# A fused attention step whose first gate stage is put in another order

## The chip, the cores and the metric

The kernel runs on one core of a Trainium2 chip. The metric is the device time of one execution in microseconds (us), the median over runs. TensorE (PE in the profile; PEld is its weight load), VectorE (DVE), ScalarE (ACT) and GpSimd (POOL) each work through a queue of their own in order; SyncE (SP) issues most of the transfers (DMA). A semaphore wait holds up everything behind it on the same engine.

## The reference, cut to what matters

One layer of a diffusion backbone: a modulated RMSNorm, one projection whose columns go to two groups of heads, two attentions, gates, an output projection.

```python
shift, scale, gate = modulation(c, w_mod[l], b_mod[l])           # silu(c) @ w_mod + b_mod
h = rmsnorm(xs, norm_gain[l]) * (1.0 + scale) + shift
q_a, k_a, v_a, g_a, q_b, k_b, v_b, g_b = project(h, w_in[l], ...)  # h @ w_in, then split
...
xs = xs + gate * merge_out(o_a, g_a, o_b, g_b, w_out[l])         # (o * silu(g)) @ w_out
```

There are 1152 tokens of width 1024: 128 context tokens (tile 0) and 1024 latent ones (tiles 1 to 8, 128 tokens each). The change concerns only the first piece of work: the norm, the modulation, and the products that give `g_a`, the gates of the first group.

## The kernel before, in words

Products are made nearly exact in three parts. A weight block of 128 rows and 512 columns, `raw` k (k from 0 to 7, named rawga in the trace), is split into a rounded high part (whiga, a cast on ACT) and the rest (wloga, a subtraction). Values h are split likewise: a high part by ACT, `h(0)`, then an exact copy hf by DVE and a low part by POOL, `h(1)`. A product is high by high, low weight by high, and high by low value.

The first stage goes over the rows of the inner dimension in steps. Step j prepares slice j of the modulation and the values, and multiplies with slice k = j - 1:

- A tile of tokens is loaded (xn), squared with its sum on ACT (sq, `squares`), the reciprocal root is taken on POOL (rsx), the tile is scaled on DVE (`scaled`), turned by eight transposes on PE (px, `turned_tile`), and copied to xT (`keep`: the first half on ACT, the second on DVE). Tiles 1 to 4 are done before the steps, the others inside them: 5 and 6 in steps 1 and 2, then 7, 8 and 0 by the table `rest`.
- `modulate_rows(j)` multiplies the slice wm of `w_mod` with the conditions (pm, 16 matmuls) and copies the rows (mrows); `modulate(j)` turns them (2 matmuls, L374) and makes the scale a_mod and the shift b_col.
- `modulated(j, 1, 4, 0)` makes the values of slice j for tiles 1 to 4 from xT (L433 on ACT, L436 on DVE, L437 on POOL). `modulated(k, 5, 2, 0)` does so for tiles 5 and 6, and the table `second` gives those of tiles 7, 8 and 0.
- `first_gates` multiplies four column groups (ch 0 to 3) with tiles 1 to 4 into four banks (pg_f, 512 wide; L267, L271, L272); `next_gates` those of tiles 5 and 6 (pg_s, 256 wide) from step 3 on.

`W_GA.split` makes both parts of one weight block and then issues the load of a later block; there are three buffers for raw blocks, three for wm and four for tiles, so a load waits until the buffer's last reader is done. All loads stand in one list on SP. `warm(n)` issues matmuls that nobody reads. The order of each engine's queue is the order in which the code is written: `in_order` at the end fixes it.

After this stage come the other projections and the attention, which hold most of the time and which the change leaves as they are.

Of the kernel before, what the change touches and what calls it, by code (L numbers as in the profile page):

```python
# [13 lines left out]
ALU = mybir.AluOpType  # L14
# [4 lines left out]
P = 128  # L19
D = 1024  # L20
KT = D // P
# [37 lines left out]
QUERY_AT = (0, 2, 3, 6)  # L59
PAD = 2  # L60
SECOND_FROM = 5
WARM = (12, 5, 2, 2, 4)
LOADLEAD = 5
OUTRATE = 2.5
PADRATE = 3
POOL_LO = ("gb",)
# [49 lines left out]
def hybrid_step(ctx, tc, x_prompt, x_sample, cache_k_a, cache_v_a, cache_k_b, cache_v_b,  # L116
# [3 lines left out]
    nc = tc.nc  # L120
# [94 lines left out]
    class Weights:  # L215
# [19 lines left out]
            for _ in range(sum(n for _, n in set(self.pools))):  # L235
                self.load()

        def split(self, eng=None):
            k = len(self.hi)
            h = wp.tile([P, 512], F32R, tag="whi", name=f"whi{self.tag}_{k}")  # L240
            l = wp.tile([P, 512], F32R, tag="wlo", name=f"wlo{self.tag}_{k}")
            nc.scalar.copy(h, self.raw[k])
            eng = eng or (nc.gpsimd if self.tag in POOL_LO and k % 2 else nc.vector)
            eng.tensor_tensor(l, self.raw[k], h, op=ALU.subtract)
            self.hi.append(h)
            self.lo.append(l)
            self.load()

    W_QA = Weights([(CQ[0], 512)], "qa")
    W_QB = Weights([(CQ[1], 512)], "qb")  # L250
# [10 lines left out]
    def gate_products(out, w, ch, ts, k, first=True, last=True, part=None):  # L261
        cs = slice(P * ch, P * ch + P)
        if part != 1:
            gate_high(out, w, cs, ts, k, first)
        if part != 0:
            i, to = third(ts)
            nc.tensor.matmul(out, w.hi[k][:, cs], h_at(1, i, k, to), start=False, stop=(k == KT - 1 and last))  # L267
# [54 lines left out]
    with tc.tile_pool(name="st", bufs=2, side="right") as st:  # L322
# [9 lines left out]
        def load_wm(j):  # L332
            w = st.tile([P, KT, 2, P], F32, tag="wm", name=f"wm{j}", bufs=3)
            for ks in (slice(0, 4), slice(4, 8)) if j == 0 else (slice(0, 8),):
                nc.sync.dma_start(w[:, ks], w_mod_ss[j][:, ks])
            wm.append(w)
# [20 lines left out]
        def modulate_rows(j, half=2):  # L357
            if half != 1:
                pmod[j] = bank_tr(f"pm{j}")
            pm = pmod[j]  # L360
            for k in range(4 * (half == 1), 4 if half == 0 else KT):
                a = 32 * (k % 4)
                nc.tensor.matmul(pm[a : a + 32, 0:256], sil32[:, k, :], wm[j][:, k].rearrange("p s n -> p (s n)"),
                                 start=(k < 4), stop=(k >= 4), tile_position=(0, a))
            if half == 0:
                return
            mrows[j] = st.tile([P, 256], F32, tag="mrows", name=f"mrows{j}")
            (nc.scalar.copy if j > 1 else nc.vector.tensor_copy)(mrows[j], pm[:, 0:256])

        def modulate(j):  # L370
            pm = pmod.pop(j)[:, 256:512]
# [17 lines left out]
        def load_x(t):  # L389
            xe[t] = st.tile([P, D + 32], F32, tag="xn", name=f"xn{t}", bufs=4)  # L390
            xn[t] = xe[t][:, 0:D]
            nc.sync.dma_start(xn[t], x_tile[t])
# [17 lines left out]
        def turned_tile(t, tags, between=None):  # L410

            for c in range(2):
                px[t, c] = bank(tags[c], f"px{t}_{c}")
                for i in range(4):
                    if c and i == 2 and between:
                        between()
                    k = 4 * c + i
                    nc.tensor.transpose(px[t, c][:, P * i : P * i + P], xn[t][:, P * k : P * k + P], ident)

        def keep(t, c, copy, a=0, b=4):  # L420
            at = slice(P * place(t), P * place(t) + P)
            copy(xT[:, 4 * c + a : 4 * c + b, at], px[t, c].rearrange("p (k n) -> p k n", n=P)[:, a:b])

        def modulated(j, t0, n, cond):

            w = P * n
            dst = slice(P * place(t0), P * place(t0) + w)
            i, to = third(dst)
            a, b = (x[:, j, cond : cond + 1] for x in (a_mod, b_col))
            hf = st.tile([P, 512], F32, tag="hf", name=f"hf{j}_{t0}", bufs=3)  # L430
            h = h_at(0, i, j, to)
            s = w // 2 if (j, t0) == (0, 1) else w
            nc.scalar.activation(h[:, 0:s], xT[:, j, dst][:, 0:s], AF.Identity, scale=a, bias=b)  # L433
            if s < w:
                nc.vector.tensor_scalar(h[:, s:w], xT[:, j, dst][:, s:w], a, b, op0=ALU.mult, op1=ALU.add)
            nc.vector.tensor_scalar(hf[:, :w], xT[:, j, dst], a, b, op0=ALU.mult, op1=ALU.add)  # L436
            nc.gpsimd.tensor_tensor(h_at(1, i, j, to), hf[:, :w], h_at(0, i, j, to), op=ALU.subtract)  # L437

# [3 lines left out]
        load_wm(0)  # L442
        W_GA.load()
        load_wm(1)
        load_x(5)
        W_GA.load()
        load_x(6)
        load_wm(2)
        W_GA.load()
        load_wm(3)  # L450

# [3 lines left out]
            for _ in range(n):  # L455
                nc.tensor.matmul(idle, blank, blank.unsqueeze(1).to_broadcast([P, 4, P]), start=True, stop=True)

        second = [x for k in range(KT) for x in ((k, 7, 2, 0), (k, 0, 1, 1))]

        def first_gates(ch, k, part=None):  # L460
            gate_products(big[ch], W_GA, ch, slice(0, 512), k, part=part)

        def next_gates(ch, k):
            o = 256 * (ch % 2)
# [32 lines left out]
        keep(2, 1, copies[1])  # L497
        keep(3, 1, copies[0])
        modulate_rows(0)
        W_GA.split(nc.gpsimd)  # L500
        turned_tile(4, "AB", lambda: modulate(0))
        keep(4, 0, copies[0], 0, 1)
        modulated(0, 1, 4, 0)
        keep(4, 0, copies[0], 1, 4)
        keep(4, 1, copies[1])
        load_x(7)
        squares(5)
        warm(WARM[4])
        big = [bank("ABAB"[ch], f"pg0_{ch}_f") for ch in range(4)]
        sg_tile.append(lambda n: st.tile([P, 512], F32, tag="sg", name=n))  # L510
        rest = {3: 7, 4: 8, 5: 0}

        late = {1: 8, 2: 0}

        for j in range(1, KT + 3):
            big_on, small_on = j <= KT, 3 <= j
            if 1 < j < KT:
                W_GA.split()
            if j == KT + 1:
                put_gates(big[0], 0, 0, slice(0, 512))  # L520
            if j == 1:
                for part in (W_GA.hi, W_GA.lo):
                    for ch in range(3):
                        nc.tensor.matmul(big[ch], part[0][:, P * ch : P * ch + P], h_at(0, 0, 0, slice(0, 512)),
                                         start=(part is W_GA.hi), stop=False)
            elif big_on:
                first_gates(0, j - 1, 0)
                first_gates(1, j - 1, 0)
                if j == KT:
                    first_gates(2, j - 1, 0)  # L530
            if j == 3:
                small = [bank("C", f"pg0_{ch}_s") for ch in (0, 2)]
            if j < KT:
                modulate_rows(j)
                if j + 3 < KT:
                    load_wm(j + 3)
                if j in late:
                    load_x(late[j])
            if j in (1, 2):
                scaled(4 + j)  # L540
            if j == 1:
                W_GA.split()
            if j in rest:
                scaled(rest[j])
            if j + 1 in rest:
                squares(rest[j + 1])
            if big_on:
                first_gates(0, j - 1, 1)
                first_gates(1, j - 1, 1)
                first_gates(2, j - 1, 1 if j in (1, KT) else None)  # L550
            if j < KT:
                modulate(j)
                modulated(j, 1, 4, 0)
                if j == 1:
                    squares(6)
            if big_on:
                first_gates(3, j - 1)
            if j in (1, 2):
                turned_tile(4 + j, ("CC", "DE")[j - 1])
                for c in range(2):  # L560
                    keep(4 + j, c, copies[c])
            if j == 2:
                for k in range(2):
                    modulated(k, 5, 2, 0)
            if j in rest:
                turned_tile(rest[j], "DE")
                for c in range(2):
                    keep(rest[j], c, copies[c])
            if 1 < j < KT:
                modulated(j, 5, 2, 0)  # L570
            for ch in range(4):
                if small_on:
                    next_gates(ch, j - 3)
                if j > SECOND_FROM or (j == SECOND_FROM and ch % 2):
                    more()
            if KT - 2 <= j < KT:
                raw = st.tile([P, KT, 2, P], F32, tag="wm", name=f"raw_qa{j}", bufs=3).rearrange(
                    "p (k a) s n -> p k (a s n)", a=2)
                k0 = 4 * (j - KT + 2)
                c0, n = W_QA.cols[0]  # L580
                nc.sync.dma_start(
                    raw, w_in[P * k0 : P * k0 + 512, c0 : c0 + n].rearrange("(k p) n -> p k n", p=P))
                W_QA.raw += [raw[:, k] for k in range(4)]
# [902 lines left out]
```

## Time and profile before

| what | value |
|---|---|
| median of 3 runs | 704.12 us (702.76 to 704.14) |
| the profiled execution | 705.18 us, span of its instructions 703.5 us |
| PE busy | 693.2 us, 99% of the span |
| DVE, ACT, POOL busy | 464.3, 410.7, 338.5 us |
| PE share of the chain that ended last | 94% |

The profile's times count from the first instruction. A row of its timeline gives start, duration, engine, line, operation, output and inputs, and in brackets how long the engine had stood idle and what it waited for. A row of the chain gives start, length and the work that decided. "PEclk" is the share of its full clock that PE was granted.

### The profile page before, as it was taken

The numbers are of one execution on the slowest core, as the hardware profiler recorded it, in microseconds if no ns is written. First come the engines' busy times: TensorE is split into PE (matmuls) and PEld (weight loads), VectorE is DVE, ScalarE is ACT, GpSimd is POOL, SyncE is SP. The second block draws the span as 40 slices with busy tenths as digits, with TensorE's granted clock in tenths as the row PEclk, the third lists the DMA queues.
The fourth block names the chain that finished last, engine by engine and source line by source line (L and its number), as shares of the span: only waits on it lengthen the run. The fifth ranks groups of instructions, "written<-read, shape, count | busy, mean of one in ns | idle before, by whom it ended". The sixth has DMA issues, their size and how long they took to land.

```text
span 703.5 us, 10690 instructions
## 1 busy us (share of the span) xinstructions
PE 693.2 (99%) x3546; PEld 560.6 (80%) x3546; DVE 464.3 (66%) x1008; ACT 410.7 (58%) x850; POOL 338.5 (48%) x357
## 2 busy tenths in 40 slices
PE   8899999999999999999999999999999999999997
PEld 4578988878788889987878787888887888887876
DVE  4678247877787773757777567567675775775563
ACT  6556412312233242178787877787778778877770
POOL 4447013332222240259676654665575557456751
PEclk9899999999999999999999999999999999999999
DMA  8952273349445016431222121212221221212323
GB/s 344 396 188 89 96 283 88 84 93 297 118 122 150 1 61 192 149 113 57 82 76 91 46 83 54 66 62 76 68 76 39 69 89 46 83 53 91 98 75 121
DMA packets 53336, 78.51 MB, mean 112 GB/s; under 512 B 6952, under 2 KB 25496, under 8 KB 52384
## 3 DMA queue, kind: packets, MB, share of 16 engines
q1 hardware_dynamic: 45040, 65.86, 28.1%
q10 hardware_dynamic: 8240, 11.96, 6.4%
q8 instruction: 28, 0.46, 0.3%
q14 instruction: 28, 0.23, 0.1%
HBM read 58.63 MB, written 19.18 MB: 111 GB/s over the span
## 4 chain that ended last, share of the span: by engine, by line
PE 94%; DMA 2%; ACT 1%; DVE 1%; issue 0%; POOL 0%; ACTq 0%; DVEq 0%
PE po L1332 14%; PE pv L1254 7%; PE pv L1251 7%; PE st L1230 5%; PE pmx L941 5%; PE pv L1253 5%; PE st L1231 5%; PE pq L259 5%; PE pq L257 5%; PE pq L258 5%; PE st L1225 4%; PE pg L267 3%; PE pg L271 3%; PE pg L272 3%; PE pk L258 2%; PE pk L259 2%
## 5 line engine op out<-in xcount | busy, mean ns | idle before, releaser
L1241 POOL TENSOR_TENSOR pl<-pe,ph 128x512 fp32r<-128x512 f32 x130 | 168.7, 1299 | 134.7 <-DVE nm L997 65.5
L942 DVE TENSOR_REDUCE mx<-pmx 128x1 f32<-128x384 f32 x192 | 101.0, 552 | 55.3 <-PE pmx L941 53.1
L1233 ACT ACTIVATE pe<-st 128x512 f32<-128x512 f32 x146 | 86.9, 595 | 28.4 <-PE st L1231 27.6
L1237 ACT CAST ph<-pe 128x512 fp32r<-128x512 f32 x146 | 90.6, 621 | 4.8
L1251 PE MATMUL pv<-ph,v_hi 128*128 128x512 f32 x208 | 82.3, 396 | 0.1
L1254 PE MATMUL pv<-pl,v_hi 128*128 128x512 f32 x208 | 82.1, 395 | 0.2 <-DVE pl L1227 0.2
L997 DVE CUSTOM_DVE_ANT_0 sn<-sn,mask,nsink 128x512 f32<-128x512 f32 (+1 forms) x64 | 46.3, 724 | 42.0 <-PE sn L994 40.6
L1332 PE MATMUL po<-wo,ogh 128*128 128x512 f32 (+1 forms) x224 | 73.3, 388 | 0.0
L182 POOL TENSOR_TENSOR rs_q<-ms_q,mhalf 128x8 f32<-128x8 f32 x18 | 34.2, 1898 | 80.8 <-DVE ms_q L180 80.8
L941 PE MATMUL pmx<-kha,qt 128*128 128x384 f32 x192 | 60.4, 362 | 0.0
L1230 PE MATMUL st<-qt,kha 128*128 128x512 f32 x144 | 57.8, 402 | 0.0
L1253 PE MATMUL pv<-ph,v_lo 128*64 128x512 f32 x146 | 57.7, 395 | 0.0
L1231 PE MATMUL st<-qb,kla 68*128 68x512 f32 x144 | 57.3, 398 | 0.0
L1254 PEld LDWEIGHTS pv<-pl,v_hi 128*128 128x128 f32 x208 | 39.0, 188 | 17.5 <-DVE pl L1227 0.6
L983 ACT ACTIVATE pen<-sn,nm 128x512 f32<-128x512 f32 (+2 forms) x72 | 45.0, 627 | 6.7 <-DVE nm L997 3.3
L1226 ACT CAST ph<-st 128x512 fp32r<-128x512 f32 x62 | 36.4, 586 | 19.8 <-PE st L1225 17.8
L1332 PEld LDWEIGHTS po<-wo,ogh 128*128 128x128 f32 x224 | 41.1, 188 | 6.4 <-ACT ogh L1294 0.3
L1251 PEld LDWEIGHTS pv<-ph,v_hi 128*128 128x128 f32 x208 | 39.2, 189 | 7.6 <-issue 0.6
L1227 DVE TENSOR_TENSOR pl<-st,ph 128x512 fp32r<-128x512 f32 x62 | 42.4, 686 | 3.0 <-ACT ph L1226 2.5
L700 ACT CAST qo0q<-ptq 128x512 fp32r<-128x512 f32 x18 | 10.6, 586 | 57.9 <-PE ptq L697 57.9
L1332 PE MATMUL po<-wo,ogl 128*128 128x512 f32 (+1 forms) x112 | 43.6, 389 | 0.0
L941 PEld LDWEIGHTS pmx<-kha,qt 128*128 128x128 f32 x192 | 35.4, 190 | 4.5
(245 smaller groups left out, 1707.2 us busy)
## 6 DMA issues: line engine op xcount, KB each, us to landing
qt<-qd SPq DMA_DIRECT2D x36, 256.0 KB, 3.0
wm<-in_w_mod_ss_dram SPq DMA_DIRECT2D x7, 1024.0 KB, 12.2
qd<-qo0q ACTq DMA_DIRECT2D x36, 128.0 KB, 2.4
qd<-qo1q ACTq DMA_DIRECT2D x36, 128.0 KB, 2.4
sgl<-gd SPq DMA_DIRECT2D x35, 128.0 KB, 2.4
out_dram<-yt SPq DMA_DIRECT2D x17, 256.0 KB, 2.1
xn<-in_x_sample_dram SPq DMA_DIRECT2D x8, 512.0 KB, 6.2
wg<-in_w_mod_g_dram SPq DMA_DIRECT2D x4, 1024.0 KB, 8.7
```

The lines of the kernel that those rows point to most:

```text
L258: nc.tensor.matmul(out, h_at(0, i, k, tok), w.lo[k], start=False, stop=False)
L941: nc.tensor.matmul(pm[:, 0:384], lhs, kha[:, g, 3 * b : 3 * b + 3, :], start=True, stop=True)
L942: nc.vector.tensor_reduce(mx[:, h, b : b + 1], pm[:, 0:384], axis=AX.X, op=ALU.max)
L1230: nc.tensor.matmul(s, kh, qtile[i], start=True, stop=False)
L1231: nc.tensor.matmul(s, kl, qbtile[i], start=False, stop=True)
L1233: nc.scalar.activation(pe, s, AF.Exp)
L1237: nc.scalar.copy(ph, pe)
L1241: nc.gpsimd.tensor_tensor(pl, pe, ph, op=ALU.subtract)
L1251: nc.tensor.matmul(pv, two, ph, start=(b == 0), stop=False)
L1253: nc.tensor.matmul(pv[0:64, :], vl, ph, start=False, stop=False)
L1254: nc.tensor.matmul(pv, two, pl, start=False, stop=last)
L1332: nc.tensor.matmul(po[n, q.start], a, wo_parts[KT * n + k][lo][:, q], start=(k == KS[0] and p == 0), stop=(k == KS[-1] and p == 2))
```

## The change

All edits are in the first stage, and what is computed stays:

- The load of raw block 1 stands ahead of tile 5's, and wm slice 2 ahead of tile 6's.
- `split` can be made in two pieces. The first low part goes from POOL to DVE and stands behind the first values of slice 0.
- Ahead of step 1, ACT copies a piece of tile 4 before it casts weight block 0, and the two turning matmuls of slice 0 come after four of tile 4's transposes in place of six.
- The values of slice 1 are made half by ACT, half by DVE, as those of slice 0 were.
- Tiles 5 and 6 are squared and turned both in step 2; tiles 7, 8 and 0 are turned in steps 4, 5 and 6 (before: 3, 4, 5), and squared one step later, behind the values of that step.
- In step 1 the products with slice 0 are put as high, slice 1 of the modulation, low weights, low values. In step 2 all four column groups have their high and low weight products before slice 2 of the modulation.
- The rows of slice 2 are copied by DVE. The warming matmuls are 12, 6, 2, 1, 5 in place of 12, 5, 2, 2, 4.
- The order in `second` follows the tiles: those of slices 0 and 1 for tiles 7 and 8 come first.

```diff
-WARM = (12, 5, 2, 2, 4)
+WARM = (12, 6, 2, 1, 5)
...
-            (nc.scalar.copy if j > 1 else nc.vector.tensor_copy)(mrows[j], pm[:, 0:256])
+            (nc.scalar.copy if j > 2 else nc.vector.tensor_copy)(mrows[j], pm[:, 0:256])
...
-            s = w // 2 if (j, t0) == (0, 1) else w
+            s = w // 2 if j < 2 and t0 == 1 else w
             nc.scalar.activation(h[:, 0:s], xT[:, j, dst][:, 0:s], AF.Identity, scale=a, bias=b)
             if s < w:
                 nc.vector.tensor_scalar(h[:, s:w], xT[:, j, dst][:, s:w], a, b, op0=ALU.mult, op1=ALU.add)
+            if between:
+                between()
             nc.vector.tensor_scalar(hf[:, :w], xT[:, j, dst], a, b, op0=ALU.mult, op1=ALU.add)
...
-        W_GA.split(nc.gpsimd)
-        turned_tile(4, "AB", lambda: modulate(0))
-        keep(4, 0, copies[0], 0, 1)
-        modulated(0, 1, 4, 0)
+        def first_values():
+            keep(4, 0, copies[0], 0, 1)
+            W_GA.split_high()
+            modulate(0)
+
+        turned_tile(4, "AB", first_values)
+        modulated(0, 1, 4, 0, W_GA.split_low)
...
-        rest = {3: 7, 4: 8, 5: 0}
+        rest = {4: 7, 5: 8, 6: 0}
...
-            if 1 < j < KT:
+            if j == 2:
+                squares(6)
+                W_GA.split_high()
+                scaled(5)
+            elif 2 < j < KT:
                 W_GA.split()
...
+                for ch in range(3):
+                    one_gate(ch, W_GA.lo[0], False)
+                modulate(1)
+                modulated(1, 1, 4, 0)
+                squares(5)
             if j in rest:
                 scaled(rest[j])
+            if big_on:
+                first_gates(0, j - 1, 1)
+                first_gates(1, j - 1, 1)
+                first_gates(2, j - 1, 1 if j in (1, 2, KT) else None)
+            if 1 < j < KT:
+                modulate(j)
+            if j == 2:
+                scaled(6)
+                W_GA.split_low()
+            if 1 < j < KT:
+                modulated(j, 1, 4, 0)
             if j + 1 in rest:
                 squares(rest[j + 1])
```

On ACT, from the cast of weight block 1 in step 1 to the values of slice 2; sq5 is the square of tile 5, h0_0_2 the high values of slice 2 for tiles 1 to 4. Before:

```order
L242 CAST whiga_1_380<-rawga_1_196 128x512
L382 ACTIVATE b_col_150<-m4_1_391,colt_163 128x2
L433 ACTIVATE h0_0_1_117<-xT_174,b_col_150,a_mod_149 128x512
L401 ACTIVATE sq6_399,ms6_400<-xn6_198 128x1025
L422 COPY xT_174<-px5_0_407 128x4x128
L242 CAST whiga_2_419<-rawga_2_202 128x512
L368 COPY mrows2_438<-pm2_429 128x256
L401 ACTIVATE sq7_445,ms7_446<-xn7_342 128x1024
L433 ACTIVATE h0_0_2_118<-xT_174,b_col_150,a_mod_149 128x512
```

And now:

```order
L241 CAST whiga_1_372<-rawga_1_194 128x512
L389 ACTIVATE b_col_150<-m4_1_383,colt_163 128x2
L440 ACTIVATE h0_0_1_117<-xT_174,b_col_150,a_mod_149 128x256
L408 ACTIVATE sq5_392,ms5_393<-xn5_196 128x1025
L408 ACTIVATE sq6_403,ms6_404<-xn6_200 128x1025
L241 CAST whiga_2_408<-rawga_2_202 128x512
L440 ACTIVATE h0_0_2_118<-xT_174,b_col_150,a_mod_149 128x512
```

The square of tile 7 no longer stands ahead of the values of slice 2, and the copy of slice 2's rows has left ACT; tile 6's square now stands ahead of the cast of weight block 2.

On PE, from the last product of slice 0 to the rows of slice 2 (pm2); px5 is tile 5 being turned. Before:

```order
L267 MATMUL pg0_3_f_357<-h1_0_0_124,whiga_0_312 128x512
L418 MATMUL px5_0_407<-ident_162,xn5_194 128x128 x4
L418 MATMUL px5_1_412<-ident_162,xn5_194 128x128 x4
L271 MATMUL pg0_0_f_354<-h0_0_1_117,whiga_1_380 128x512
L272 MATMUL pg0_0_f_354<-h0_0_1_117,wloga_1_381 128x512
L271 MATMUL pg0_1_f_355<-h0_0_1_117,whiga_1_380 128x512
L272 MATMUL pg0_1_f_355<-h0_0_1_117,wloga_1_381 128x512
L363 MATMUL pm2_429<-wm2_200,sil32_172 32x256 x8
```

And now:

```order
L274 MATMUL pg0_3_f_353<-h1_0_0_124,whiga_0_319 128x512
L278 MATMUL pg0_0_f_350<-h0_0_1_117,whiga_1_372 128x512
L279 MATMUL pg0_0_f_350<-h0_0_1_117,wloga_1_374 128x512
L278 MATMUL pg0_1_f_351<-h0_0_1_117,whiga_1_372 128x512
L279 MATMUL pg0_1_f_351<-h0_0_1_117,wloga_1_374 128x512
L278 MATMUL pg0_2_f_352<-h0_0_1_117,whiga_1_372 128x512
L279 MATMUL pg0_2_f_352<-h0_0_1_117,wloga_1_374 128x512
L278 MATMUL pg0_3_f_353<-h0_0_1_117,whiga_1_372 128x512
L279 MATMUL pg0_3_f_353<-h0_0_1_117,wloga_1_374 128x512
L370 MATMUL pm2_419<-wm2_198,sil32_172 32x256 x8
```

Tile 5's transposes have left this place (they now stand with tile 6's at the end of step 2), and four more products stand ahead of pm2.

On SP, the loads behind wm slice 1; xn5 and xn6 are tiles 5 and 6. Before:

```order
L392 DMA xn5_194<-in_x_sample_dram 128x1024
L230 DMA rawga_1_196<-in_w_in_dram 128x512
L392 DMA xn6_198<-in_x_sample_dram 128x1024
L335 DMA wm2_200<-in_w_mod_ss_dram 128x2048
L230 DMA rawga_2_202<-in_w_in_dram 128x512
```

And now:

```order
L230 DMA rawga_1_194<-in_w_in_dram 128x512
L399 DMA xn5_196<-in_x_sample_dram 128x1024
L342 DMA wm2_198<-in_w_mod_ss_dram 128x2048
L399 DMA xn6_200<-in_x_sample_dram 128x1024
L230 DMA rawga_2_202<-in_w_in_dram 128x512
```

Two pairs have changed places; the load of weight block 2 behind them stands where it stood.

More of the change, by code (lines that the diff above doesn't have):

```diff
@@ L236, in load_all, with split_high, split_low, split @@
                 self.load()
-        def split(self, eng=None):
+        def split_high(self):
             k = len(self.hi)
             h = wp.tile([P, 512], F32R, tag="whi", name=f"whi{self.tag}_{k}")
+            nc.scalar.copy(h, self.raw[k])
+            self.hi.append(h)
+        def split_low(self):
+            k = len(self.lo)
             l = wp.tile([P, 512], F32R, tag="wlo", name=f"wlo{self.tag}_{k}")
[L242 to L245, printed above, removed]
+            eng = nc.gpsimd if self.tag in POOL_LO and k % 2 else nc.vector
+            eng.tensor_tensor(l, self.raw[k], self.hi[k], op=ALU.subtract)
             self.lo.append(l)
             self.load()
+        def split(self):
+            self.split_high()
+            self.split_low()
     W_QA = Weights([(CQ[0], 512)], "qa")
@@ L414, in turned_tile @@
                 for i in range(4):
-                    if c and i == 2 and between:
+                    if c and i == 0 and between:
                         between()
@@ L422, in keep, with modulated @@
             copy(xT[:, 4 * c + a : 4 * c + b, at], px[t, c].rearrange("p (k n) -> p k n", n=P)[:, a:b])
-        def modulated(j, t0, n, cond):
+        def modulated(j, t0, n, cond, between=None):
             w = P * n
@@ L444, in hybrid_step @@
         load_wm(1)
+        W_GA.load()
         load_x(5)
-        W_GA.load()
+        load_wm(2)
         load_x(6)
-        load_wm(2)
         W_GA.load()
@@ L456, in warm, with one_gate @@
                 nc.tensor.matmul(idle, blank, blank.unsqueeze(1).to_broadcast([P, 4, P]), start=True, stop=True)
-        second = [x for k in range(KT) for x in ((k, 7, 2, 0), (k, 0, 1, 1))]
+        second = [(0, 7, 2, 0), (1, 7, 2, 0), (0, 0, 1, 1), (1, 0, 1, 1)]
+        second += [x for k in range(2, KT) for x in ((k, 7, 2, 0), (k, 0, 1, 1))]
         def first_gates(ch, k, part=None):
             gate_products(big[ch], W_GA, ch, slice(0, 512), k, part=part)
+        def one_gate(ch, w, first):
+            nc.tensor.matmul(big[ch], w[:, P * ch : P * ch + P], h_at(0, 0, 0, slice(0, 512)), start=first, stop=False)
         def next_gates(ch, k):
@@ L506, in hybrid_step @@
         load_x(7)
-        squares(5)
         warm(WARM[4])
@@ L521, in hybrid_step @@
             if j == 1:
[L522 to L525, printed above, removed]
+                for ch in range(3):
+                    one_gate(ch, W_GA.hi[0], True)
             elif big_on:
[L527 to L530, printed above, removed]
+                for ch in range(4 if j == 2 else 2 + (j == KT)):
+                    first_gates(ch, j - 1, 0)
             if j == 3:
@@ L538, in hybrid_step @@
                     load_x(late[j])
-            if j in (1, 2):
-                scaled(4 + j)
             if j == 1:
                 W_GA.split()
+                for ch in range(3):
+                    one_gate(ch, W_GA.lo[0], False)
+                modulate(1)
+                modulated(1, 1, 4, 0)
+                squares(5)
             if j in rest:
                 scaled(rest[j])
+            if big_on:
[9 more added lines that the diff above has]
+                modulated(j, 1, 4, 0)
             if j + 1 in rest:
@@ L547, in hybrid_step @@
             if big_on:
[L548 to L559, printed above, removed]
+                first_gates(3, j - 1, 1 if j == 2 else None)
+            if j == 2:
+                turned_tile(5, "CC")
                 for c in range(2):
-                    keep(4 + j, c, copies[c])
-            if j == 2:
+                    keep(5, c, copies[c])
+                turned_tile(6, "DE")
+                for c in range(2):
+                    keep(6, c, copies[c])
                 for k in range(2):
```

## The prediction

> **What bounds the kernel now.** I read the granted clock and busy times by stretches first, then the chain of work that ended last, then the timeline of its first 40 us. The stretches show where PE, the bound, is not at work (columns: stretch, length, busy time of PE, PEld, DVE, ACT and POOL with instructions, PE's clock, the transfer engines' share, GB/s):
>
> ```profile
> 21.44:24.85 3.41, 3.41 (x28) 2.16 (x27) 1.67 (x4) 1.47 (x5) 0.94 (x2) 1.00 1.03 410
> 24.85:28.26 3.41, 1.12 (x10) 0.79 (x7) 1.52 (x4) 1.32 (x3) 0.08 (x1) 1.00 1.00 411
> 28.26:31.68 3.42, 2.83 (x12) 1.56 (x16) 2.38 (x4) 3.10 (x6) 3.04 (x5) 0.50 1.07 420
> 31.68:35.09 3.41, 3.41 (x18) 2.00 (x11) 2.13 (x2) 1.42 (x3) 2.22 (x4) 0.50 0.96 330
> 60.00:700.00 640.00, 638.69 (x3179) 523.92 (x3177) 427.54 (x936) 375.67 (x781) 311.03 (x314) 1.00 0.31 95
> ```
>
> From 60 us on PE is idle for 1.31 us in 640: whatever PE gains ahead of that comes out at the end. Ahead of it there is one hole, where PE works 1.12 us of 3.41, and behind the hole two stretches at half clock. The transfer engines are full throughout, at 410 to 420 GB/s. The chain of waits names the hole's cause:
>
> ```profile
> 14.57 12.27 DMA xn<-in_x_sample_dram
> 26.94 1.15 ACT sq L401 x2
> 28.09 0.71 ACT h L433
> 28.85 0.80 PE pg_f L271
> ```
>
> The transfer of tile 7 is issued at 14.57 and lands 12.27 us later. ACT's queue holds its square, and behind it the values of slice 2, which need nothing of tile 7. PE waits for those values. The timeline says how long, and when step 4 begins:
>
> ```profile
> 28.85 0.80 PE L271 MATMUL pg_f<-h,whiga 128*128 128x512 f32 x1 [2.88 <-ACT h L433]
> ...
> 32.59 1.21 DVE L408 TENSOR_SCALAR xn<-xn,rsx 128x1024 f32<-128x1024 f32 x1
> ...
> 35.99 1.03 PE L418 MATMUL px<-ident,xn 128*128 128x128 f32 x8
> ...
> 38.29 0.40 PE L271 MATMUL pg_f<-h,whiga 128*128 128x512 f32 x1
> ```
>
> The last row is the first product with slice 3: my mark. The two rows between price the half clock. Tile 7 was scaled at 33.80 and could be turned then; PE came to it at 35.99. So the slow clock costs at most 2.2 us; the rest of that stretch is DVE and POOL at work.
>
> A rule bears on the clock. The Trainium skill, TensorE: Matmul & The Clock Gate, Part 1, says that a free-running window of about 3.4 us is watched, that an idle window halves the clock and a busy one releases it, and that the phase differs from run to run. The trace agrees on the grid (the two stretches at 0.50 are 6.83 us together, two windows), and differs in that a window with 1.12 us of work dropped it and one with 2.83 did not release it. By this page the drop may be missing in some of the timed runs of before, and then those have 2.2 us less to lose: the sum of the second rival below.
>
> **The change, part by part.** I follow PE from its first real product to the mark. Prices of PE at full clock, from the chain's steps (start to next start):
>
> ```profile
> 35.22 0.22 PE pm L374 x2
> ...
> 36.15 0.87 PE px L418 x8
> ...
> 37.38 0.12 PE pg_s L271
> ...
> 38.45 0.23 PE pg_f L271
> ...
> 39.39 1.00 PE pm L363 x16
> ```
>
> *The first low part to DVE, the copy ahead of the cast.*
>
> ```profile
> 12.74 1.27 POOL L244 TENSOR_TENSOR wloga<-rawga,whiga 128x512 fp32r<-128x512 f32 x1 [1.24 <-ACT whiga L242]
> ...
> 13.35 0.30 ACT L382 ACTIVATE b_col<-m,colt 128x2 f32<-128x2 f32 x1 [0.70 <-DVE m L376]
> 13.37 0.67 DVE L378 TENSOR_SCALAR a_mod<-m,bsc,colt 128x2 f32<-128x2 f32 x1
> ...
> 14.13 0.60 ACT L433 ACTIVATE h<-xT,b_col,a_mod 128x256 fp32r<-128x256 f32 x1 [0.33 <-DVE a_mod L378]
> 14.78 0.96 PE L524 MATMUL pg_f<-h,whiga 128*128 128x512 f32 x3 [0.66 <-ACT h L433]
> ```
>
> a_mod takes 0.67 us and ends just as POOL's subtraction does (14.01); later it takes 0.29 (below). Without POOL at work it ends 0.38 earlier, at 13.66. On ACT the small copy now goes ahead of the cast, and the shift b_col behind both ends at about 13.75. Values 0.60: first product at 14.45, a gain of 0.33. The low part costs DVE 0.69 from 14.1, ready at 14.9; PE now asks for it only after pm1, at 16.15. Hidden, with 1.2 us to spare. The warming matmuls (one more, one less, one more) fill idle time of PE: nothing.
>
> *Steps 1 and 2.* The rows that give the durations:
>
> ```profile
> 17.50 0.42 DVE L368 COPY mrows<-pm 128x256 f32<-128x256 f32 x1 [1.90 <-PE pm L363]
> ...
> 18.51 0.69 DVE L244 TENSOR_TENSOR wloga<-rawga,whiga 128x512 fp32r<-128x512 f32 x1
> ...
> 19.11 0.17 DVE L376 TENSOR_REDUCE m<-pm 128x4 f32<-128x16 f32 x1
> ...
> 19.31 0.29 DVE L378 TENSOR_SCALAR a_mod<-m,bsc,colt 128x2 f32<-128x2 f32 x1
> ...
> 20.41 1.05 ACT L401 ACTIVATE sq<-xn 128x1025 bf16<-128x1025 f32 x1
> 20.56 0.50 PE L271 MATMUL pg_f<-h,whiga 128*128 128x512 f32 x1 [0.44 <-ACT h L433]
> ...
> 21.75 0.59 PEld L363 LDWEIGHTS pm<-wm,sil 128*32 128x32 f32 x16 [0.43 <-DMA wm<-in_w_mod_ss_dram]
> 21.84 0.54 POOL L405 TENSOR_TENSOR rsx<-ms,mhalf 128x1 f32<-128x1 f32 x1
> 22.40 0.62 ACT L242 CAST whiga<-rawga 128x512 fp32r<-128x512 f32 x1 [0.38 <-DMA rawga<-in_w_in_dram]
> ...
> 23.66 0.75 DVE L408 TENSOR_SCALAR xn<-xn,rsx 128x1024 f32<-128x1024 f32 x1
> ...
> 28.00 0.80 ACT L433 ACTIVATE h<-xT,b_col,a_mod 128x512 fp32r<-128x512 f32 x1
> ```
>
> PE from 14.45: three products 0.70, pm1 1.00, three 0.70, two turning matmuls 0.22, six products 1.39: 18.46. Slice 1's values by then: rows copied 0.42 behind pm1 (16.2 to 16.65), low weights 0.69 (17.35), a reduction of 0.17, a_mod 0.29 (17.8), and half the values 0.60, since DVE takes the other half: 18.47. PE waits for nothing (before: 0.44 us, until 20.56). Eight products, 1.86: 20.35.
>
> Then pm2, which needs wm2. Before, PE waited for it until 21.75, and tile 6 had landed by 20.41, where its square began without waiting. Now wm2 has tile 6 (512 KB) behind it in place of ahead of it: at 410 GB/s that is 1.3 us, so 20.4 for wm2. Tile 6 takes wm2's old place in the byte stream: 21.7. The bounds: no later than 20.41 and a whole wm2 of 2.6 us, 23.0; no earlier than matters, 21.0. I take 21.7, since the stream is full and the bytes ahead are the same.
>
> PE: pm2 1.00 (21.4), three products 0.70, turning 0.22, one product 0.23 (22.55), tile 5 turned 0.87 (23.4). Tile 5's square now follows slice 1's values and its scaling ends by 21.4: hidden. ACT: square of tile 6 from 21.7, 1.15 with its sum (22.9), cast of block 2 0.62 (23.45; it had landed at 22.4), values of slice 2 0.80: 24.25. **Before they ended at 28.80; this is where the time comes from.** The copy of slice 2's rows, moved to DVE, is done by 21.9, before PE turns them. DVE: root 0.54 on POOL (23.5), scaling of tile 6 0.75 (24.35), low weights 0.69 (25.0). So PE waits about 0.95 us for tile 6, from 23.4 to 24.4, turns it (25.3), and has slice 2's values and weights ready: four products 0.93, pm3 1.00, five 1.16, turning 0.22, three 0.70, twelve small ones 1.43: **30.7** at the mark.
>
> Step 3 has a thin margin. DVE copies two tiles, makes three exact copies and the low weights of block 3 there, and POOL three low parts in turn with it; from the lengths that these took before (29.30 to 32.67 in the timeline, 3.4 us) they end near 29.1, slice 3's values at 30.5. That is 0.2 us before PE asks.
>
> *Tiles 7, 8, 0 one step later.* Tile 7 is turned in step 4, so the mark of before must be cut by its 0.87. Their squares now stand behind the values that PE waits for. In step 6 tile 0's scaling stands ahead of the reduction for slice 6, 0.75 us on DVE; DVE has some idle time there, so I charge 0.2 (0 to 0.5). The order in `second` and the later load of block 5 move nothing that PE asks for before it comes: nothing.
>
> *The sum.* 38.29 - 0.87 - 30.7 - 0.2 = 6.5 us, of which 2.2 is the clock: no idle stretch of PE is left that is over 1 us. The bounds of tile 6's landing give 5.2 (at 23.0) and 6.8 (at 21.0). Against the profiled execution's own 705.18 us that is 698.7; against the median of the runs, 704.12, it is 697.6. The profiled execution is 2.4 us above the fastest run shown (702.76), as much as the clock's price; I can't tell which of the timed runs paid it, and take the middle, **698.1**.
>
> **The rivals.**
>
> *The transfers become the bound.* PE comes to every load 6.5 us earlier, and the stream is full. For: tile 7 took 12.27 us, and the transfer of block 4 is as slow (issued at 19.22 with the next, 12.1 us to landing).
>
> ```profile
> 19.22 4.88 SPq L230 DMA_DIRECT2D rawga<-in_w_in_dram  x2
> ...
> rawga<-in_w_in_dram SPq DMA_DIRECT2D x1, 256.0 KB, 12.1
> ```
>
> It landed at 31.3; ACT, behind the square of tile 7, now asks for it at about 32.0. Against: 0.7 us of margin, and more for all others. If the stream runs 2 to 3 us late for the earlier asking, the gain is 3.5 to 4.5: 700.1.
>
> *The clock is not in the median's runs.* Then before paid only the hole: 6.5 - 2.2 = 4.3, 699.8. For: the spread of the runs. Against: the hole's cause, a transfer, is there in every run, and the median is nearer to the profiled run than the fastest is.
>
> *Tile 6 takes tile 7's place* (the other side). Its square now stands ahead of the cast and values that PE needs. Each us of landing after 21.7 is paid once, and from a hole of 2.9 us on the clock drops too, 2.2 more. It decides at 26.0: 4.3 us of hole, and 2.2. With tile 7's 12.27 us from its issue near 9.7 it would be at 22.0, so it would need 4 us more: 704.5 if it lands at 26.2.
>
> *Nothing measurable.* The wait moves on to low weights and values of slice 3 on DVE and POOL (the thin margin) and eats the gain: 703.5. It needs 6 us there, where their whole work is 3.4.
>
> **How the numbers follow.** Forecast 0.62; transfers 0.14; clock absent 0.14; nothing 0.06; tile 6 slower 0.04. A measurement of this kernel tells changes over about 0.2% (1.4 us) from none. Faster: 0.62 + 0.14 + 0.14 = 0.90; same 0.06; slower 0.04. The range goes from 696.0 (the larger gain, 6.8, from the median, and a run as far below it as the fastest was) to 700.5, which takes in the two rivals at 700.1 and 699.8 and leaves out the last two.
>
> **What would show it.** Right: the first row of ACT's values of slice 2 ends near 24.2 with no wait for tile 7 ahead of it; PE's longest wait after 15 us is about 1 us, for tile 6's scaling; the clock stays 1.00 from 5 us on; the first product with slice 3 is near 30.7; PE's idle time after 60 us stays near 1.3 us. Wrong: a wait of ACT's square of tile 6 beyond 23 us, a stretch with 0.50 behind it, or waits of PE for slice 3's values or for wm slices in steps 3 to 5.

## The result, and the profile after

| | before | after |
|---|---|---|
| median (lowest to highest) | 704.04 us (702.76 to 704.67), 6 runs | 699.44 us (698.51 to 699.71), 6 runs |
| profiled execution (span) | 705.18 us (703.5 us) | 698.51 us (696.8 us) |
| first product with slice 3, the mark | 38.29 us | 31.06 us |

The ratio is 0.9934 (95% interval 0.9921 to 0.9946). The medians are 4.60 us apart, the two profiled executions 6.67. The forecast was 698.1 with a range of 696.0 to 700.5. Its sum, 6.5 us, is right for the two profiled executions and too large for the medians; most of the experiments are about that difference.

The stretches of after, with the columns of those of before:

```profile
21.44:24.85 3.41, 3.01 (x29) 2.15 (x18) 2.51 (x7) 2.79 (x5) 0.58 (x1) 1.00 1.01 405
24.85:28.26 3.41, 3.41 (x31) 2.25 (x30) 3.41 (x8) 3.11 (x7) 2.38 (x3) 1.00 1.01 414
28.26:31.68 3.42, 3.42 (x23) 3.07 (x22) 2.57 (x6) 1.65 (x2) 2.33 (x3) 1.00 1.02 411
60.00:693.30 633.30, 632.36 (x3143) 518.81 (x3141) 421.31 (x925) 370.67 (x772) 305.65 (x308) 1.00 0.31 96
```

Where PE worked 1.12 of 3.41 us it now works all the time, and the half clock behind it is gone. The last stretch is cut 3.5 us ahead of the span's end, as that of before was; PE is idle for 0.94 us of it (before 1.31), so no wait has been put off to the rest of the program. The transfers run at the same 405 to 414 GB/s.

The list of PE's waits between 12 and 62 us had two lines before, 3.3 us and 0.7 us. Of after it has one:

```profile
PE px L425 <- DVE xn L415: 0.4, 1, 0.4
```

The timeline, at the places that the forecast named:

```profile
14.41 0.96 PE L474 MATMUL pg_f<-h,whiga 128*128 128x512 f32 x3
...
20.82 0.59 PEld L370 LDWEIGHTS pm<-wm,sil 128*32 128x32 f32 x16 [0.35 <-DMA wm<-in_w_mod_ss_dram]
21.78 1.06 ACT L408 ACTIVATE sq<-xn 128x1025 bf16<-128x1025 f32 x1 [2.00 <-DMA xn<-in_x_sample_dram]
...
23.01 0.58 POOL L412 TENSOR_TENSOR rsx<-ms,mhalf 128x1 f32<-128x1 f32 x1 [2.03 <-ACT sq L408]
...
23.46 0.22 DVE L391 TENSOR_SCALAR b_col<-m,colt 128x2 f32<-128x2 f32 x1
23.62 0.75 DVE L415 TENSOR_SCALAR xn<-xn,rsx 128x1024 f32<-128x1024 f32 x1
23.72 0.81 ACT L440 ACTIVATE h<-xT,b_col,a_mod 128x512 fp32r<-128x512 f32 x1 [0.28 <-DVE b_col L391]
24.53 1.06 PE L425 MATMUL px<-ident,xn 128*128 128x128 f32 x8 [0.40 <-DVE xn L415]
25.35 0.47 PE L278 MATMUL pg_f<-h,whiga 128*128 128x512 f32 x1
...
31.06 0.40 PE L278 MATMUL pg_f<-h,whiga 128*128 128x512 f32 x1
...
63.46 0.34 PE L278 MATMUL pg<-h,whiga 128*128 128x384 f32 x1
```

The values of slice 2 end at 24.53 in place of 28.80, and nothing of tile 7 stands ahead of them. The last row is the first product of the next column group. Before, it stood here:

```profile
69.75 0.34 PE L271 MATMUL pg<-h,whiga 128*128 128x384 f32 x1
```

So 6.29 us are gained by then, and 0.4 in all that follows. In the other experiments I use this row as a second mark, since it stands behind the whole reordered stage.

### The profile page after: what moved, and what is told of

It is laid out like the page before. It is cut to its first block, busy times and chain, and to the rows that moved or that the text cites. A ratio compares the mean times of both kernels' runs of the same rounds, so it can differ in the third digit from the quotient of the medians.

```text
span 696.8 us, 10695 instructions
## 1 busy us (share of the span) xinstructions
PE 690.7 (99%) x3547; PEld 559.4 (80%) x3547; DVE 463.3 (66%) x1011; ACT 410.0 (59%) x849; POOL 336.7 (48%) x356
## 4 chain that ended last, share of the span: by engine, by line
PE 96%; DMA 1%; ACT 1%; DVE 1%; SPq 0%; issue 0%; ACTq 0%
PE po L1354 14%; PE pv L1276 7%; PE pv L1273 7%; PE st L1252 5%; PE pmx L963 5%; PE st L1253 5%; PE pv L1275 5%; PE pq L266 5%; PE pq L264 5%; PE pq L265 5%; PE st L1247 4%; PE pg L278 3%; PE pg L274 3%; PE pg L279 3%; PE pk L265 2%; PE pk L266 2%
```

## The experiments

### What the kernel before pays from run to run

Nothing is edited here: the kernel before, once more.

> The kernel before once more, for the granted clock of each run. Theory (the clock's price differs between runs): a run that holds the half-clock stretch of 6.8 us has a mean clock of 0.995 (1 - 0.5 x 6.83/703.5), one without has 1.00, and the two differ by up to 2.2 us: the profiled 705.18 belongs to the first, the median of 704.04 to a mixture. Rival (all runs hold it, and the 1.1 us between the profiled run and the median are something else): every run shows 0.995.

12 runs gave 703.50 us (702.70 to 704.69), beside 703.84 for 23 more runs of the same kernel on the same chip. The run that was profiled took 703.32, and its stretches are these:

```profile
24.85:28.26 3.41, 1.92 (x14) 1.51 (x12) 1.83 (x5) 1.36 (x3) 0.12 (x1) 1.00 1.02 420
28.26:31.68 3.42, 2.87 (x23) 1.76 (x24) 2.42 (x4) 3.39 (x8) 3.04 (x5) 1.00 1.05 412
```

The timeline of the same run:

```profile
15.64 0.97 PE L524 MATMUL pg_f<-h,whiga 128*128 128x512 f32 x3 [0.62 <-ACT h L433]
...
28.81 0.50 PE L271 MATMUL pg_f<-h,whiga 128*128 128x512 f32 x1 [2.04 <-ACT h L433]
...
67.74 0.34 PE L271 MATMUL pg<-h,whiga 128*128 128x384 f32 x1
```

The hole is at the same place and ends at the same time (28.81 against 28.85), but it is 2.04 us long and not 2.9, and the clock stays at 1.00 behind it. The second mark comes at 67.74 in place of 69.75: 2.0 us, the forecast's price of the clock (at most 2.2), is missing here.

Each run lists the mean clock of its execution, and the 60 runs of the kernel before that have it, on three chips, fall into groups by it:

| mean clock | runs | mean time | above the first group |
|---|---|---|---|
| .999 or 1.0 | 19 | 703.15 us | |
| .997 or .998 | 35 | 703.91 us | 0.76 us |
| .995 | 6 | 705.12 us | 1.97 us |

Half a clock for one stretch of 3.41 us takes 0.0024 off the mean of 703.5 us, and two stretches take 0.0049; so by their means the middle group had half a clock for one such stretch and the last for two. The profiled execution of before (705.18, mean clock .995) belongs to the last group, and the median run pays 0.8 us. The groups overlap (the middle one has a run of 703.38 and the first one of 703.87), so the clock isn't all that differs between runs.

### The kernel after, again

> The changed kernel once more. Its six runs fell at 698.5 (two) and 699.4 to 699.7 (four), the profiled one at 698.51. Theory: the 1 us between them comes from the start, where the clock is released at another point of its window, so the mean clock differs by a few thousandths and a second trace shows another release time than 4.49 us. Rival: a transfer of the first stage lands later in some runs; then the clock is the same and the trace shows a PE wait in step 2 or 3 that is about 1 us longer than the 0.40 us seen.

6 runs gave 699.30 us (698.83 to 699.70), ratio 0.9935 (0.9922 to 0.9948). The mean clock was .999 or 1.0 in all of them. That alone does not rule the theory out: in the first profiled run of this kernel and in this one the traces record the release of the clock at 4.49 and at 6.13 us, another time as the theory said, and the mean is 1.0 in both. But the release does not order the starts. The kernel before, released at 4.36 in the run above, has its first product at 15.64, and the kernel after in the last experiment, released at 5.52, has it at 14.24. The profiled run here took 699.52 us, 1.0 more than the first one of this kernel. Its timeline:

```profile
8.07 1.06 ACT L408 ACTIVATE sq<-xn 128x1025 bf16<-128x1025 f32 x1 [1.15 <-DMA xn<-in_x_sample_dram]
...
15.32 0.96 PE L474 MATMUL pg_f<-h,whiga 128*128 128x512 f32 x3
...
64.34 0.34 PE L278 MATMUL pg<-h,whiga 128*128 128x384 f32 x1
```

In the faster run the same square of tile 3 had no wait:

```profile
6.88 1.06 ACT L408 ACTIVATE sq<-xn 128x1025 bf16<-128x1025 f32 x1
```

The square of tile 3, which waits for that tile's transfer, starts 1.2 us later in one run than in the other. The first product is then 0.91 us later, and the second mark 0.88. The cause is a wait, but one of ACT at the start, and neither theory nor rival had it. It is not rare: in 5 of the 13 profiles of all kernels here this square waited 1.0 to 1.4 us. The kernel before had the same late start in the run above (first product at 15.64, against 14.78) and paid nothing for it: its slice 2 began at 28.81, since tile 7 set that time and not PE. The hole had hidden the late start.

### The late squares alone

```diff
-        rest = {3: 7, 4: 8, 5: 0}
+        rest = {4: 7, 5: 8, 6: 0}
...
-            if j + 1 in rest:
-                squares(rest[j + 1])
...
+                if j + 1 in rest:
+                    squares(rest[j + 1])
```

The kernel before, with only this: the squares stand behind the values of the step, and `second` is as in the kernel after.

> The kernel before with one part of the change alone: tiles 7, 8, 0 squared behind the values of their step and turned one step later. Theory (this part makes the gain; all the rest is covered by the landing of tile 6 and the step's own work): by the rows, values of slice 2 at 25.2 to 26.0, the first product with slice 3 near 31.4 against 31.06 in the changed kernel: 0.4 to 0.7 us slower than the changed kernel, 700.0, that is 4.0 us under before. Rival (the parts add up: first low part 0.33, slice 1's values 2.0 less tile 5's 0.9): 1.5 to 2 us slower than the changed kernel, 701.2.

699.78 us (699.25 to 700.91), ratio 0.9944 (0.9930 to 0.9957): all but 0.3 to 0.5 us of what the whole change brings. PE's waits behind 12 us:

```profile
PE pg_f L525 <- ACT h L433: 0.6, 1, 0.6
PE pg_f L271 <- ACT h L433: 0.4, 1, 0.4
PE pm L363 <- DMA wm<-in_w_mod_ss_dram: 0.2, 1, 0.2
```

The wait of 2.9 us is gone, the two of before ahead of it stand. The clock stays at 1.00.

### Everything but the late squares

The reverse of that edit, in the kernel after.

> The changed kernel with that part alone undone: tiles 7, 8, 0 squared ahead of the values and turned in steps 3, 4, 5 as before. Theory: ACT waits for tile 7 until 26.9 again, values of slice 2 at 28.9, PE idle for about 3.4 us; everything won ahead of it is lost in that wait: the time of before within 0.5 us, 704.0. Rival (the rest of the change is worth 1.5 us or more by itself): 702.5 or less.

703.92 us (702.87 to 705.23), ratio 1.0003 (0.9993 to 1.0012): nothing is left of the gain. The timeline:

```profile
14.82 0.97 PE L473 MATMUL pg_f<-h,whiga 128*128 128x512 f32 x3
...
26.88 1.06 ACT L408 ACTIVATE sq<-xn 128x1024 bf16<-128x1024 f32 x1 [3.45 <-DMA xn<-in_x_sample_dram]
27.93 0.80 ACT L440 ACTIVATE h<-xT,b_col,a_mod 128x512 fp32r<-128x512 f32 x1
28.78 0.50 PE L278 MATMUL pg_f<-h,whiga 128*128 128x512 f32 x1 [2.83 <-ACT h L440]
```

Products with slice 2 begin at 28.78, as before. The other parts gain nothing ahead of them here: the first product comes at 14.82 (before 14.78; tile 3's square waited 0.33 us in this run), and the hole is 2.83 us long (before 2.88, expected 3.4). The clock groups are there again: .995 with 704.70 to 705.23, .999 with 702.87 and 702.91. The profiled run is the one of 702.87, and PE is at work for 1.06 us of the stretch, as little as in the profile of before (1.12), yet the clock stays:

```profile
24.85:28.26 3.41, 1.06 (x8) 0.86 (x8) 2.15 (x4) 1.39 (x3) 0.15 (x1) 1.00 0.99 406
28.26:31.68 3.42, 2.90 (x23) 1.76 (x24) 1.74 (x3) 3.39 (x7) 3.04 (x5) 1.00 1.04 417
```

So it isn't the hole's length that decides on the drop. The traces show what does: how the hole lies against the clock's windows. In the profile of before the clock is released at 4.37 us and drops at 28.26, seven windows of 3.413 us later, so the stretch from 24.85 to 28.26 is one of its windows. (So it is in the run of before above, released at 4.36, which has 1.92 us of work in it and no drop.) Here the clock is released at 6.79 and drops, behind the last product, at 699.69, 203 windows later. So a window ends at 27.27, in the middle of the hole, and each of the two windows that share the hole has more work:

```profile
23.85:27.27 3.42, 1.74 (x15) 1.30 (x13) 3.15 (x7) 0.40 (x1) 0.00 (x0) 1.00 1.02 419
27.27:30.68 3.41, 1.90 (x20) 1.09 (x20) 0.96 (x3) 3.38 (x7) 2.19 (x4) 1.00 1.04 417
```

Counted so in all 13 profiles, from each run's own release, the clock dropped behind windows with 0 to 1.14 us of PE work and behind none with 1.71 or more.

### Which half of the late squares: the place in the queue, or the step

```diff
             if j in rest:
                 scaled(rest[j])
-            if j + 1 in rest:
-                squares(rest[j + 1])
...
+                if j + 1 in rest:
+                    squares(rest[j + 1])
```

The kernel before, with the squares behind the values but tiles 7, 8 and 0 turned in steps 3, 4 and 5 as they were.

> The kernel before, with the squares of tiles 7, 8 and 0 behind the values of their step, but turned in steps 3, 4, 5 as before. Theory (taking the square from the head of ACT's queue is not enough: the tile must be turned a step later too, since tile 7's scaling on DVE stands ahead of the reduction for slice 3, behind a square that can't start before 26.9): values of slice 2 at 26, but the first product with slice 3 still near 35: 702.2. Rival (ACT's queue was all): 700.0.

701.66 us (701.58 to 702.30), ratio 0.9971 (0.9959 to 0.9982): half of it. The timeline shows what still holds:

```profile
25.51 0.81 ACT L433 ACTIVATE h<-xT,b_col,a_mod 128x512 fp32r<-128x512 f32 x1 [1.91 <-DVE b_col L384]
26.90 1.06 ACT L401 ACTIVATE sq<-xn 128x1024 bf16<-128x1024 f32 x1 [0.58 <-DMA xn<-in_x_sample_dram]
27.96 0.56 ACT L422 COPY xT<-px 128x512 f32<-128x512 f32 x1
28.58 1.07 PE L363 MATMUL pm<-wm,sil 128*32 128x256 f32 x16 [1.01 <-ACT xT L422]
...
32.74 1.09 PE L418 MATMUL px<-ident,xn 128*128 128x128 f32 x8 [0.64 <-DVE m L376]
```

The values are free at 25.51, but now the copy of a turned tile stands behind the square and PE's pm3 waits 1.01 us for it. The second wait, 0.64 us ahead of tile 7's turning, is there in the kernel before too when its clock stays full (0.65 us in its second profile). With both moves neither is left: the place in the queue gave 2.2 us (703.83 to 701.66), the step the other 1.9 (to 699.78, measured on another chip).

### The hole filled

```diff
             elif big_on:
+                if j == 3:
+                    warm(13, "C")
                 first_gates(0, j - 1, 0)
```

The kernel before with 13 matmuls in the hole that nobody reads (`warm` takes the bank's tag).

> The kernel before, with 13 matmuls that nobody reads put on PE in the hole ahead of slice 2's products (they use a free bank; nothing else moves). Theory (part of before's time is the clock dropping in the hole, in some runs for no window, one or two): no run shows a mean clock under 0.999, the runs above 703.6 vanish, median 703.0, the hole itself stays. Rival (the half clock is covered by DVE and POOL, whose work bounds that stretch): median unchanged at 703.8.

703.13 us (702.80 to 704.16, 11 runs), beside 703.83; ratio 0.9996 (0.9987 to 1.0005), an interval that also allows no change at all. The clock did what the theory says, .999 or 1.0 in each of the 11 runs, against 5 of the 16 runs of before beside them:

```profile
25.68 2.97 PE L456 MATMUL idle<-blank 128*128 128x512 bf16 x13
28.59 0.50 PE L271 MATMUL pg_f<-h,whiga 128*128 128x512 f32 x1
```

The 0.70 us between the medians fit the 0.76 of the table. But four runs stand at 703.7 to 704.2 with a full clock: about 1 us of spread in the kernel before has another cause, which I did not find.

### The old order of loads

```diff
-        W_GA.load()
         load_x(5)
-        load_wm(2)
+        W_GA.load()
         load_x(6)
+        load_wm(2)
```

The kernel after, with this.

> The changed kernel with the loads in the old order (tile 5, weight block 1, tile 6, wm slice 2). Theory (wm2 then lands at 21.6 in place of 20.6 and PE, which asks at 20.7, waits; tile 6 lands 2 us earlier, for which nothing hurries): 0.6 to 0.9 us over the changed kernel, 700.2. Rival (the order inside a full stream doesn't matter, the last of the two lands at the same time): 699.4.

699.79 us (699.38 to 699.96), ratio 0.9942 (0.9930 to 0.9955): 0.35 to 0.5 more than after, between theory and rival. The kernel after was not run beside it, and its own median went from 698.61 to 699.44 between occasions, so a difference of this size is not firm. The timeline shows the cause that was expected:

```profile
22.17 1.07 PE L370 MATMUL pm<-wm,sil 128*32 128x256 f32 x16 [0.59 <-DMA wm<-in_w_mod_ss_dram]
...
25.82 1.06 PE L425 MATMUL px<-ident,xn 128*128 128x128 f32 x8 [0.36 <-DVE xn L415]
```

The wait for wm2 is the one the theory named, at 0.59 us. The wait for tile 6's scaling did not shrink by as much, though tile 6 had landed well before. The next experiment shows why.

### The two parts on slices 0 and 1

```diff
             W_GA.split_high()
+            W_GA.split_low(nc.gpsimd)
             modulate(0)
...
-        modulated(0, 1, 4, 0, W_GA.split_low)
+        modulated(0, 1, 4, 0)
...
-            s = w // 2 if j < 2 and t0 == 1 else w
+            s = w // 2 if j < 1 and t0 == 1 else w
```

The kernel after, with the first low part back on POOL and the values of slice 1 by ACT alone.

> The changed kernel with two parts undone: the first low part on POOL at its old place, slice 1's values by ACT alone. Theory (tile 6, landing at 21.7, sets the start of step 3, so work ahead of it is covered): 0 to 0.3 us over the changed kernel, 699.5. Rival (each pays its term of the sum, 0.33 for the low part and 0.2 for the values): 700.0, with the first product near 14.8 and PE's wait for tile 6 still near 0.4.

700.07 us (699.68 to 700.62), ratio 0.9947 (0.9935 to 0.9960): 0.6 to 0.8 more, as the rival said, though against medians from other occasions again. Then each alone, beside the kernel after on the same chip:

> The changed kernel with the first low part alone put back on GpSimd, at its old place; the values of slice 1 stay shared by ScalarE and VectorE. Theory: of the .6 to .75 us that the two parts cost together this one costs most, because the subtraction on GpSimd stands beside the scale a_mod and stretches it (0.67 against 0.29 us), so that the first product comes about 0.4 us later, and every product behind it: 699.8, against 699.4 for the changed kernel itself. Rival: the wait for tile 6's scaling (0.4 us) covers it: 699.4.

> The changed kernel with the values of slice 1 by ScalarE alone; the first low part stays on VectorE. Theory: ScalarE needs about 0.80 us for all of them against 0.60 for half, so TensorE waits about 0.2 us ahead of slice 1's products and then as much less for tile 6's scaling, which sets the end of step 2: 699.4 to 699.6, with a wait of 0.1 to 0.3 us at the first product of slice 1 and one of 0.2 to 0.4 at tile 6's transposes. Rival: this part alone costs .6 or more (700.0), since the later values also hold ScalarE up ahead of the square of tile 6.

> The changed kernel once more, beside the two kernels with one part undone, on the same chip: 699.3 to 699.5, and the spread between about 698.5 and 699.7 that was put down to the landing of tile 3 at the start.

| | median | ratio to before |
|---|---|---|
| after | 698.61 us (698.35 to 699.19) | 0.9926 (0.9914 to 0.9939) |
| first low part on POOL | 699.14 us (699.00 to 699.26) | 0.9933 (0.9919 to 0.9946) |
| values of slice 1 by ACT | 698.66 us (698.62 to 699.34) | 0.9929 (0.9917 to 0.9942) |

The expectations were set from the earlier medians of the kernel after (699.30 and 699.44). Here it runs 0.7 to 0.8 us lower: four of its five runs stand at 698.35 to 698.75, where the runs without the late start stood. So the differences are what counts. The low part costs 0.5 us. The values cost 0.05, which can't be told from nothing, and the wait expected at the first product of slice 1 is not there. With POOL:

```profile
13.40 1.27 POOL L248 TENSOR_TENSOR wloga<-rawga,whiga 128x512 fp32r<-128x512 f32 x1 [1.96 <-ACT whiga L241]
...
13.61 1.21 DVE L442 TENSOR_SCALAR h<-xT,a_mod,b_col 128x256 fp32r<-128x256 f32 x1
...
14.97 0.93 PE L474 MATMUL pg_f<-h,whiga 128*128 128x512 f32 x3 [0.55 <-DVE h L442]
...
22.80 0.55 POOL L412 TENSOR_TENSOR rsx<-ms,mhalf 128x1 f32<-128x1 f32 x1 [1.30 <-ACT sq L408]
...
24.10 0.75 DVE L415 TENSOR_SCALAR xn<-xn,rsx 128x1024 f32<-128x1024 f32 x1
```

And the kernel after beside it:

```profile
13.60 0.41 DVE L442 TENSOR_SCALAR h<-xT,a_mod,b_col 128x256 fp32r<-128x256 f32 x1
...
14.24 0.97 PE L474 MATMUL pg_f<-h,whiga 128*128 128x512 f32 x3
```

DVE's half of the first values ends at 14.82, just behind POOL's subtraction (14.67), and takes 1.21 us in place of 0.41; the first product is 0.73 us later, the run 0.5 us. The theory had the cause and named the wrong victim: in before it was a_mod that was stretched (0.67 against 0.29). The last two rows with POOL show that the rival was wrong as well: tile 6's root is ready at 23.35, but its scaling starts at 24.10. The scaling stands on DVE behind the reduction, a_mod and b_col of slice 2, which follow PE's own pm2. When PE comes late, this scaling does too, so the wait of 0.4 us cannot take up what was lost ahead of it. The experiments that undid something ahead of it (the loads, both parts, each part) all kept a wait of 0.36 us there.

## Why the prediction was right, point by point

*What bounds it.* Right, and shown from both sides: the late squares alone bring nearly all, everything else without them nothing.

*The first product.* 14.41 against 14.45. The reason holds too: the experiment that puts the subtraction back on POOL loses 0.73 us there (the forecast's term was 0.33, for a_mod alone). The costing of the low part on DVE at nothing was right: no wait of PE stands there.

*Steps 1 and 2.* "PE waits for nothing" was right but for about 0.2 us until pm2, which came at 20.82 in place of 20.35: the first product with slice 1 took 0.41 us, where 0.23 is usual, and its values had ended at 18.73 (forecast 18.47). The other terms that were too small stand behind the blocks of pm. The chain of after gives them:

```profile
18.87 0.41 PE pg_f L278
...
20.89 1.00 PE pm L370 x16
21.89 0.91 PE pg_f L274 x3
22.80 0.23 PE pm L381 x2
...
25.59 0.23 PE pg_f L278
...
27.52 0.67 PE pg_f L274 x2
```

Three products right behind pm take 0.91 and not the 0.70 that I had from products elsewhere. The chain of before had shown it, two products behind pm at full clock, and I passed it over:

```profile
40.39 0.66 PE pg_f L267 x2
```

Tile 6 landed where it was put (its square began at 21.78, forecast 21.7), and its scaling ended at 24.37 (forecast 24.35). PE waited 0.40 us for it and not 0.95, only because it came later itself. The products with slice 2 began at 25.35 (forecast 25.3), so the errors cancelled there. That is luck. And the cause of the wait was hardly the transfer, as the forecast had it: b_col ends at 23.68 and the root at 23.59, but where the root was ready well ahead the wait was still 0.36 us. So tile 6's landing holds PE for about 0.04 us, and the rest is the path from PE's own pm2 through DVE.

*Step 3 and the mark.* 31.06 against 30.7. Here the extra 0.2 behind pm3 has no wait to vanish in. The thin margin held: slice 3's values began at 30.03 and ended at 30.85 (forecast 30.5), and PE did not wait.

*Tiles 7, 8, 0 later.* Charged 0.2. From the mark to the second mark before needed 69.75 - 38.29 = 31.46 us; after needs 32.40 less 0.87 for tile 7: 0.07 more.

*The sum.* 38.29 - 0.87 - 31.06 - 0.07 = 6.29, and 0.4 behind it: 6.7 between the profiled executions, 6.5 in the forecast. For the medians it failed in the step that chose the time: "I can't tell which of the timed runs paid it, and take the middle". Of the clock's 2.0 us the median run of before pays 0.8, so 1.2 us of the sum was never there to win in the median. The measured 699.44 is nearer to the second rival's 699.8 than to the forecast's 698.1. That rival, that the clock is not in the median's runs at all, was half right, and its chance of 0.14 was too small. What spoke against it, that the hole is in every run, is true of the hole and not of the clock: a hole of 2.88 us dropped it in one run, and one of 2.83, cut in two by the end of a window, did not in another. That is also what is wrong with the forecast's "from a hole of 2.9 us on the clock drops too". By the rule in the Trainium skill, TensorE: Matmul & The Clock Gate, Part 1, the phase of the window differs from run to run. These runs agree: the release comes between 4.36 and 6.79 us in the 13 profiles, and there are two groups of prices, 0.76 and 1.97 us, beside a group with none.

*What was missing.* The late start. It costs before nothing and after 0.9 us, in 4 of the 6 runs of the result if their times (699.43 to 699.71, against 698.51 and 698.53) tell which these are; only the profiled ones show it. With it the ledger of the medians closes: 6.7 for the profiled pair, less 1.2 for the clock, less 0.9, is 4.6. (The medians stand 1.14 and 0.93 us from the profiled runs, so the two prices, measured elsewhere, fit.) That before does not pay for the late start is shown by one profiled run of it.

*The other rivals.* The transfers did not become the bound: no wait of PE for a transfer is left after 12 us. Tile 6 did not take tile 7's place.

A better version did not come out of these runs. The one wait left is 0.4 us, less than a measurement tells, and the start's 0.9 us is a transfer's.

## What to carry to other kernels

A small piece of work that waits for a transfer costs what stands behind it in the queue, not what it takes itself; put it behind all that does not need the transfer, and then look for what comes next behind it. A hole in front of the bound engine hides the jitter of everything ahead of it, so when the hole is closed that jitter becomes part of the time: price the gain from the spread of the runs, not from one profile. A cost that appears in some runs only, such as a dropped clock, belongs in the sum with its share.

## What the runs showed of the hardware

- The same hole of PE, at the same time, dropped the clock for two windows, one or none: 1.97, 0.76 and 0 us in 6, 35 and 19 of 60 runs (the number of windows is inferred from the mean clocks; the profiles show two windows and none).
- Windows of 3.413 us, counted from each run's own release of the clock (4.36 to 6.79 us in the 13 profiles), ended in a drop with 0 to 1.14 us of PE work and in none with 1.71 or more. A window with 2.83 us of work at half clock did not end the drop.
- In the first 8 us, one tile's transfer landed about 1.2 us later in some executions than in others: its square started at 8.07 and at 6.88 in two runs of one kernel, and waited 1.0 to 1.4 us in 5 of 13 profiles.
- A VectorE instruction beside a GpSimd subtraction took 1.21 us in place of 0.41, and ended just behind it.
- Products that follow a block of 16 narrow matmuls (32 columns of weights) take 0.2 us more than the same products elsewhere (three 0.91 against 0.69, two 0.67 against 0.46).
